# New places for activations and weights, and another order in the output projection, in a decoder layer that works with split float32

## The chip, the cores and the metric

The kernel runs on one core of one Trainium2 chip. The metric is the device time of one execution in microseconds: the median of three runs before the change is 1117.33 us (1116.82 to 1117.43). One more execution was profiled; all rows below are of that one.

## What is computed

One layer of a decoder, 256 tokens by 2048 channels, all float32. Cut to what matters here:

```python
h = rms_norm(x, ln_mix_pre[l])
proj = h @ w_in[l]                          # 2048 x 5648
q, k, v, z, xbc, dt_raw = jnp.split(proj, splits, axis=-1)
attn = moba_attention(...)                  # 8 heads of 128, one block of 256 tokens
ssm = mamba2_mixer(z, xbc, dt_raw, ...)     # 16 heads of 64, chunks of 128
mixed = jnp.concatenate([attn, ssm], axis=-1) @ w_out[l]    # 2048 x 2048
x = x + rms_norm(mixed, ln_mix_post[l])
h = rms_norm(x, ln_ffn_pre[l])
u = causal_depthwise_conv(h @ w_ffn_up[l], ...)             # 2048 x 11264
gate, up = jnp.split(u, [FFN_HIDDEN], axis=-1)
f = (jax.nn.gelu(gate, approximate=True) * up) @ w_ffn_down[l]   # 5632 x 2048
x = x + rms_norm(f, ln_ffn_post[l])
```

## The kernel before

**Split numbers.** Every large product is made of three: each weight and each activation is split into a part rounded to float32r ("hi") and the float32r rest ("lo"), and hi x hi, hi x lo and lo x hi are summed in PSUM. ACT rounds a weight (`whi`, L75), DVE subtracts (`wlo`, L76).

**Weights.** They come as 384 units of 128 x 1024 float32 (512 KB) in the order of use. `Weights.fetch` loads one (SP's queue, four `raw` buffers), rounds it and takes the rest. There are four buffers each for `whi` and `wlo`, and three more of each from the output projection on (`deepen`). Every unit used calls `tick`, which fetches the next unit and runs what `defer` has put off by a number of units.

**Two kinds of stages.** In a *column tile* (`cols_part`, L221 and L222; input projections of attention and part of the state-space model, and the FFN's up projection) a 128 x 128 block of the weight is loaded into the array and the activation streams: hi and lo together, 2 x 256 columns, against `whi`, then hi alone against `wlo`. Sixteen such pairs, two units, make one tile of 128 output channels. `cols_tok` (L229, L232) does the same for 128 tokens at a time, for the three tiles that begin while the second half of the tokens is not ready yet. In a *row stage* (`rows_part`, L284 to L286; v and z, the output projection, the FFN's down projection) a block of the activation is loaded and 512 columns of the weight stream; one unit gives 12 matmuls (two blocks of channels, two halves of the tokens, three products).

**Places.** The normalized activations `hT` and, for the FFN, `h2` are one tile of 128 x 16 x 2 x 256: for each block of channels, hi and then lo. The mixer's output `mT` and the gated FFN activation `gT` are two tiles each (`halves`), the lo one 32 float32 (`SHIFT`) further within 256 bytes. `Weights.place` puts the same shift ahead of the `wlo` buffers of each pool:

```python
        if n == "wlo" and pool not in self.shifted:
            self.shifted.append(pool)
            pool.tile([P, SHIFT], F32, name="gap")
```

**Order.** A scheduler orders ACT's and DVE's work by the order in which the code records it, except in the tail of the output projection, which is written by hand. The output projection has four chunks of 512 output channels. When a chunk's sums are complete, `post` squares them on ACT (for the norm), multiplies them by the norm weights on DVE (L768, L760) and makes one product of x with the next norm's weights (`x_weighted`, L763) for the second half of the tokens. Four more such products are deferred by 2 to 5 units. `rows_chunk` calls `done=post(c)` behind the last `tick` of the chunk, so behind the next unit's cast.

Of the kernel before, what the change touches and what calls it, by code (L numbers as in the profile page):

```python
# [19 lines left out]
P = 128  # L20
D = 2048
S = 256
# [33 lines left out]
class Weights:  # L56


    def __init__(self, nc, pool, units):
        self.nc, self.pool, self.units = nc, pool, units  # L60
        self.fetched, self.ready, self.more, self.base, self.behind = 0, [], None, 0, 0
        self.shifted = []

# [15 lines left out]
    def place(self, i, n, bufs, dtype):  # L79
        pool = self.pool  # L80
        if self.more and (i - self.base) % (bufs + MORE[n]) < MORE[n]:
            pool, bufs = self.more, MORE[n]
        if n == "wlo" and pool not in self.shifted:
            self.shifted.append(pool)
            pool.tile([P, SHIFT], F32, name="gap")
        return pool.tile([P, UE], dtype, name=n, tag=n, bufs=bufs)
# [35 lines left out]
def decoder_layer(ctx, tc, x, xT, win, wdt, wout, wup, wdown, relb, vec, cols, mconv, fconv,  # L122
# [11 lines left out]
    def pad(pool, name, n):  # L134
        pool.tile([P, n], F32, name=name)

    def halves(pool, name, n):

        lo = pool.tile([P, n, S], F32R, name=name + "l")
        pad(pool, name + "p", SHIFT)  # L140
        return [pool.tile([P, n, S], F32R, name=name + "h"), lo]

    def views(pair):

        return [pair[:, :, c, :] for c in range(2)]

# [6 lines left out]
    def tok(t):  # L153
        return slice(t * P, (t + 1) * P)
# [51 lines left out]
    def split_evac(dst, k, ts, ps):  # L206

        hi, lo = (d[:, k, ts] for d in dst)
        nc.scalar.copy(hi, ps)
        nc.vector.tensor_tensor(lo, ps, f32(hi), op=ALU.subtract)  # L210

    def split_scaled(dst, k, ts, src, w):

        hi, lo = (d[:, k, ts] for d in dst)
        nc.scalar.activation(hi, src, AF.Copy, scale=w)
        nc.vector.scalar_tensor_tensor(lo, src, w, f32(hi), op0=ALU.mult, op1=ALU.subtract)

    def cols_part(ps, w, aT, k, j):

        s = tok(j)  # L220
        nc.tensor.matmul(ps, w[0][:, s], aT[:, k, :, :], start=(k == 0), stop=False)  # L221
        end[0] = nc.tensor.matmul(ps[:, :S], w[1][:, s], aT[:, k, 0, :], start=False,  # L222
                                  stop=(k == KT - 1)).ins

    def cols_tok(ps, w, aT, k, j, t):

        s = tok(j)
        both = ps.rearrange("p (b c) -> p b c", b=2)[:, :, tok(t)]
        nc.tensor.matmul(both, w[0][:, s], aT[:, k, :, tok(t)], start=(t == 0 and k == 0),  # L229
                         stop=False)  # L230
        if t == NT - 1:
            nc.tensor.matmul(ps[:, :S], w[1][:, s], aT[:, k, 0, :], start=False,  # L232
                             stop=(k == KT - 1))
# [8 lines left out]
    def defer(units, fn, *args):  # L242

        pending.append([units, fn, args])
# [31 lines left out]
    def chunk_psums():  # L276
        return [acc.tile([P, 512], F32, name="pa", tag="a") for _ in range(NT)]

    def rows_part(ps, w, aT, k0, t, first, last):

        for j in range(2):
            s = chunk(j)
            a, b = (d[:, k0 + j, tok(t)] for d in aT)
            nc.tensor.matmul(ps, a, w[0][:, s], start=(first and j == 0), stop=False)  # L284
            nc.tensor.matmul(ps, a, w[1][:, s], start=False, stop=False)  # L285
            end[0] = nc.tensor.matmul(ps, b, w[0][:, s], start=False,  # L286
                                      stop=(last and j == 1)).ins

    def rows_chunk(pss, aT, kts, first=True, last=True, done=None):

        n = len(kts)
        for i in range(n):
            w = ws.take()
            for t in range(NT):
                rows_part(pss[t], w, aT, kts[i], t, first and i == 0, last and i == n - 1)
            tick()
        if done:
            for t in range(NT):
                done(t, pss[t])
# [37 lines left out]

    pad(pers, "pad0", 32)
    hT = pers.tile([P, KT, 2, S], F32R, name="hT", tag="h", bufs=1)
    pad(pers, "pad1", 32)  # L340

    with ExitStack() as mctx:
        mx = mctx.enter_context(tc.tile_pool(name="mx", bufs=1))
        mT = halves(mx, "mT", KT)

        with ExitStack() as actx:
# [7 lines left out]
            def load_x(g, n):  # L354
                nc.sync.dma_start(out=xr[:, g:g + n, :], in_=xT[:, g:g + n, :])
                for k in range(g, g + n):
                    split_scaled(views(hT), k, slice(0, S), xr[:, k, :], lnm[:, k:k + 1])

# [269 lines left out]
            for c in range(2):  # L628
                rows_chunk(chunk_psums(), views(hT), range(0, KT, 2), done=v_out(c))

# [93 lines left out]
            for c in range(2):  # L724
                rows_chunk(chunk_psums(), views(hT), range(0, KT, 2), done=gate(c))
            for h in range(2, H):
# [11 lines left out]
        for t in range(NT):  # L738
            aux(out=xt[:, t, :], in_=x[0, tok(t), :])
        pad(ctx.enter_context(tc.tile_pool(name="end", bufs=1, side="right")), "pad2", 16)  # L740
        ws.deepen(ctx.enter_context(tc.tile_pool(name="wq", bufs=1, side="right")))
# [13 lines left out]
        ss1 = pers.tile([P, NT, 4], F32, name="ss1")  # L755
        h2 = pers.tile([P, KT, 2, S], F32R, name="h2", tag="h", bufs=1)

# [7 lines left out]
        def post(c):  # L765
            def fn(t, ps):
                square_sum(ss[0][t][:, c:c + 1], ps)
                nc.vector.tensor_tensor(mm[:, t, chunk(c)], ps, wpost[:, chunk(c)], op=ALU.mult)  # L768
                weighted(t, c)
                if t == NT - 1:  # L770
                    x_weighted(t, c)
            return fn
# [22 lines left out]
        def turned(t, q):  # L795

            pt = psum("pxt").rearrange("p (j c) -> p j c", c=P)
            for j in range(4):
                nc.tensor.transpose(pt[:, j, :], ml[t][q][:, tok(j)], ident)
            dst = [h2[:, q * 4:q * 4 + 4, c, tok(t)] for c in range(2)]  # L800
            last = [nc.scalar.copy(dst[0], pt).ins]

            def rest():
                last.append(nc.vector.tensor_tensor(dst[1], pt, f32(dst[0]), op=ALU.subtract).ins)
            return rest, last
# [8 lines left out]

        for c in range(3):
            defer(2 + c, x_weighted, 0, c)
        defer(5, x_weighted, 1, 3)
        for c in range(2):
            rows_chunk(first[c], mT, hi, first=False, done=post(c))
        both = list(lo) + list(hi)  # L820
        rows_chunk(chunk_psums(), mT, both, done=post(2))
        early = [early_sum(ss[0][t][:, :3]) for t in range(NT)]
# [102 lines left out]
    fp = ctx.enter_context(tc.tile_pool(name="fp", bufs=1))  # L925
    gT = halves(fp, "gT", HALF)
    fcv = fp.tile([P, 2 * NF, 4], F32, name="fcv")
# [199 lines left out]
```

## Time and profile before

| | before |
|---|---|
| median of three runs | 1117.33 us |
| the profiled execution's own time | 1117.19 us |
| its span, first to last instruction | 1115.4 us |
| PE busy | 1108.2 us (99%) |
| DVE, ACT busy | 784.1 us (70%), 592.2 us (53%) |
| granted PE clock, mean | 0.999 |
| read from HBM | 214.44 MB |

PE's matmuls are pipelined: each is on record for longer than the distance to the next one's start. The rate is read from starts in the timeline, not from durations. "idle before" in a row is time in which the engine did nothing, and the name behind the arrow is what ended it.

### The profile page before, as it was taken

The page shows a single profiled execution, that of the slowest core. Times are in us where ns is not written, and L with a number is a line of the kernel's source. Part 1 is how long each engine was busy: PE and PEld are TensorE (multiplying, and loading weights), DVE is VectorE, ACT ScalarE, POOL GpSimd, SP SyncE. Part 2 cuts the span into 40 slices and gives each one's busy share as a digit, 9 for nine tenths or more (in the row PEclk, how much of TensorE's full clock was granted, in tenths as well). Part 3 has the DMA queues.
Part 4 walks back from the last instruction along what each step waited for, and adds up shares of the span by engine and source line. Part 5 has one row for each costly group of instructions (what it writes and reads, how often), then busy time and mean ns, then how long its engine had stood idle before and what let it go on. Part 6 is the DMA issues. An engine that isn't in the chain of part 4 may idle for free.

```text
span 1115.4 us, 15788 instructions
## 1 busy us (share of the span) xinstructions
PE 1108.2 (99%) x5888; PEld 946.6 (85%) x5888; DVE 784.1 (70%) x1270; ACT 592.2 (53%) x914; POOL 15.5 (1%) x26
## 2 busy tenths in 40 slices
PE   9999999999999999999999999999999999999997
PEld 7888888888888988888888888888888888888886
DVE  6699976776576799878777644448787878765553
ACT  6666545545454486555555444335555555554441
POOL 0010000000000000000000000000000000000000
PEclk9999999999999999999999999999999999999999
DMA  8758554555687267666556665666655656566542
GB/s 299 291 183 272 176 152 165 175 172 167 217 301 236 87 223 238 192 191 191 189 189 189 189 189 189 190 189 190 190 190 191 191 190 192 188 223 196 191 151 76
DMA packets 61356, 217.58 MB, mean 195 GB/s; under 512 B 7200, under 2 KB 8624, under 8 KB 60384
## 3 DMA queue, kind: packets, MB, share of 16 engines
q1 hardware_dynamic: 59328, 207.64, 57.6%
q0 software_dynamic: 1664, 8.59, 2.2%
q8 instruction: 46, 0.75, 0.3%
q10 hardware_dynamic: 288, 0.35, 0.1%
q14 instruction: 30, 0.25, 0.1%
HBM read 214.44 MB, written 2.11 MB: 194 GB/s over the span
## 4 chain that ended last, share of the span: by engine, by line
PE 98%; DMA 0%; SPq 0%; ACT 0%; DVE 0%; issue 0%; POOLq 0%; ACTq 0%
PE pa L221 36%; PE pa L222 18%; PE pa L285 9%; PE pa L284 9%; PE pa L286 9%; PE ph L285 4%; PE ph L284 4%; PE ph L286 4%; PE pab L221 1%; PE pa L229 1%; PE pab L222 1%; PE py L585 1%; DMA raw<-in_win_dram 0%; PE pq L229 0%; PE pa L232 0%; PE lg L675 0%
## 5 line engine op out<-in xcount | busy, mean ns | idle before, releaser
L76 DVE TENSOR_TENSOR wlo<-raw,whi 128x1024 fp32r<-128x1024 f32 (+2 forms) x389 | 469.5, 1210 | 256.9 <-ACT whi L75 249.0
L75 ACT CAST whi<-raw 128x1024 fp32r<-128x1024 f32 (+2 forms) x389 | 403.5, 1039 | 428.8 <-PE pa L221 198.2
L221 PE MATMUL pa<-h,whi 128*128 128x512 f32 x1360 | 471.7, 392 | 0.0
L222 PE MATMUL pa<-h,wlo 128*128 128x256 f32 x1360 | 382.2, 281 | 0.0
L221 PEld LDWEIGHTS pa<-h,whi 128*128 128x128 f32 x1360 | 255.3, 188 | 55.9
L222 PEld LDWEIGHTS pa<-h,wlo 128*128 128x128 f32 x1360 | 255.7, 188 | 0.0
L221 PE MATMUL pa<-hT,whi 128*128 128x512 f32 x384 | 136.7, 398 | 0.0
L222 PE MATMUL pa<-hT,wlo 128*128 128x256 f32 x384 | 107.0, 281 | 0.2 <-DVE wlo L76 0.2
L221 PEld LDWEIGHTS pa<-hT,whi 128*128 128x128 f32 x384 | 72.1, 188 | 15.7 <-issue 0.2
L943 DVE SCALAR_TENSOR_TENSOR cfc<-cfu,fcv,cfc 128x254 f32<-128x254 f32 (+1 forms) x176 | 83.2, 478 | 1.4
L222 PEld LDWEIGHTS pa<-hT,wlo 128*128 128x128 f32 x384 | 72.0, 188 | 1.2 <-DVE wlo L76 0.7
L285 PE MATMUL pa<-wlo,gTh 128*128 128x512 f32 x176 | 69.6, 396 | 0.0
L285 PE MATMUL ph<-wlo,gTh 128*128 128x512 f32 x176 | 69.6, 396 | 0.0
L284 PE MATMUL pa<-whi,gTh 128*128 128x512 f32 x176 | 69.0, 392 | 0.0
L284 PE MATMUL ph<-whi,gTh 128*128 128x512 f32 x176 | 69.0, 392 | 0.0
L286 PE MATMUL pa<-whi,gTl 128*128 128x512 f32 x176 | 68.9, 392 | 0.0
L286 PE MATMUL ph<-whi,gTl 128*128 128x512 f32 x176 | 68.9, 392 | 0.0
L941 ACT ACTIVATE cfc<-cfu,fcv 128x256 f32<-128x256 f32 x88 | 52.3, 599 | 0.2 <-DVE cfu L940 0.2
L284 PE MATMUL pa<-whi,hT 128*128 128x512 f32 x128 | 51.7, 404 | 0.0
L284 PE MATMUL pa<-whi,mTh 128*128 128x512 f32 x128 | 50.7, 396 | 0.0
L285 PE MATMUL pa<-wlo,mTh 128*128 128x512 f32 x128 | 50.6, 395 | 0.0
L286 PE MATMUL pa<-whi,hT 128*128 128x512 f32 x128 | 50.5, 394 | 0.0
(230 smaller groups left out, 1131.4 us busy)
## 6 DMA issues: line engine op xcount, KB each, us to landing
raw<-in_wup_dram SPq DMA_DIRECT2D x176, 512.0 KB, 3.5
raw<-in_wdown_dram SPq DMA_DIRECT2D x88, 512.0 KB, 3.5
raw<-in_win_dram SPq DMA_DIRECT2D x85, 512.0 KB, 3.7
raw<-in_wout_dram SPq DMA_DIRECT2D x32, 512.0 KB, 4.0
xsq<-in_x_dram SPq DMA_DIRECT2D x2, 1024.0 KB, 9.3
rows<-acd POOLq DMA_DIRECT2D x4, 512.0 KB, 8.0
xt<-in_x_dram POOLq DMA_DIRECT2D x2, 1024.0 KB, 6.8
xr<-in_xT_dram SPq DMA_DIRECT2D x6, 256.0 KB, 6.3
```

The source lines that it names most:

```text
L75: nc.scalar.copy(hi[:, s], raw[:, s])
L76: return lambda: nc.vector.tensor_tensor(lo[:, s], raw[:, s], f32(hi[:, s]), op=ALU.subtract)
L221: nc.tensor.matmul(ps, w[0][:, s], aT[:, k, :, :], start=(k == 0), stop=False)
L222: end[0] = nc.tensor.matmul(ps[:, :S], w[1][:, s], aT[:, k, 0, :], start=False, stop=(k == KT - 1)).ins
L229: nc.tensor.matmul(both, w[0][:, s], aT[:, k, :, tok(t)], start=(t == 0 and k == 0), stop=False)
L284: nc.tensor.matmul(ps, a, w[0][:, s], start=(first and j == 0), stop=False)
L285: nc.tensor.matmul(ps, a, w[1][:, s], start=False, stop=False)
L286: end[0] = nc.tensor.matmul(ps, b, w[0][:, s], start=False, stop=(last and j == 1)).ins
L585: nc.tensor.matmul(py[:, i * 64:(i + 1) * 64], rows[:, t, g, i, :], xcs[t, g][:, i * 64:(i + 1) * 64], start=True, stop=True)
L941: nc.scalar.activation(c, u, AF.Identity, scale=wv[:, 2:3], bias=wv[:, 3:4])
L943: nc.vector.scalar_tensor_tensor(c[:, sh:], u[:, :S - sh], wv[:, 2 - sh:3 - sh], c[:, sh:], op0=ALU.mult, op1=ALU.add)
```

## The change

`hT` and `h2` become two planes of 16 x 256 columns, each followed by 32 float32 of room, with the lo plane first; the first pad grows by 32 float32, so that plane 0 (lo) starts 160 bytes and plane 1 (hi) 32 bytes past a multiple of 256. The shift ahead of `wlo` is gone. `mT` and `gT` become one tile each, hi and lo side by side for each block of channels. In `cols_part` the lo summand streams first, then hi, and the matmul with `wlo` adds into the second half of the PSUM row. In the output projection, `post` is called ahead of the last `tick` of a chunk (`soon`), and the products of x are deferred by 9 to 14 units instead of 2 to 5.

```diff
@@ Weights
-        if n == "wlo" and pool not in self.shifted:
-            self.shifted.append(pool)
-            pool.tile([P, SHIFT], F32, name="gap")
...
-    def halves(pool, name, n):
-        lo = pool.tile([P, n, S], F32R, name=name + "l")
-        pad(pool, name + "p", SHIFT)
-        return [pool.tile([P, n, S], F32R, name=name + "h"), lo]
...
@@ cols_part
         s = tok(j)
-        nc.tensor.matmul(ps, w[0][:, s], aT[:, k, :, :], start=(k == 0), stop=False)
-        end[0] = nc.tensor.matmul(ps[:, :S], w[1][:, s], aT[:, k, 0, :], start=False,
+        c = slice(k * S, (k + 1) * S)
+        nc.tensor.matmul(ps, w[0][:, s], aT[:, :, c], start=(k == 0), stop=False)
+        end[0] = nc.tensor.matmul(ps[:, S:], w[1][:, s], aT[:, 1, c], start=False,
                                   stop=(k == KT - 1)).ins
@@ cols_tok
-        nc.tensor.matmul(both, w[0][:, s], aT[:, k, :, tok(t)], start=(t == 0 and k == 0),
-                         stop=False)
+        c = k * S
+        nc.tensor.matmul(both, w[0][:, s], aT[:, :, c:c + S][:, :, tok(t)],
+                         start=(t == 0 and k == 0), stop=False)
...
@@ rows_chunk
-    def rows_chunk(pss, aT, kts, first=True, last=True, done=None):
+    def rows_chunk(pss, aT, kts, first=True, last=True, done=None, soon=None):
...
+            if soon and i == n - 1:
+                for t in range(NT):
+                    soon(t, pss[t])
             tick()
...
-    pad(pers, "pad0", 32)
-    hT = pers.tile([P, KT, 2, S], F32R, name="hT", tag="h", bufs=1)
-    pad(pers, "pad1", 32)
+    pad(pers, "pad0", 64)
+    def normed(name):
+        return pers.tile([P, 2, KT * S + SHIFT], F32R, name=name, tag="h", bufs=1)
+    def summands(aT):
+        if len(aT.shape) == 4:
+            return [aT[:, :, c, :] for c in range(2)]
+        return [aT[:, c, :KT * S].rearrange("p (k s) -> p k s", s=S) for c in (1, 0)]
+    hT = normed("hT")
...
-        mT = halves(mx, "mT", KT)
+        mT = mx.tile([P, KT, 2, S], F32R, name="mT")
...
-        pad(ctx.enter_context(tc.tile_pool(name="end", bufs=1, side="right")), "pad2", 16)
+        pad(ctx.enter_context(tc.tile_pool(name="end", bufs=1, side="right")), "pad2", 48)
...
-        h2 = pers.tile([P, KT, 2, S], F32R, name="h2", tag="h", bufs=1)
+        h2 = normed("h2")
...
-                if t == NT - 1:
+                if (t, c) == (1, 2):
                     x_weighted(t, c)
...
-            dst = [h2[:, q * 4:q * 4 + 4, c, tok(t)] for c in range(2)]
+            dst = [d[:, q * 4:q * 4 + 4, tok(t)] for d in summands(h2)]
...
-        for c in range(3):
-            defer(2 + c, x_weighted, 0, c)
-        defer(5, x_weighted, 1, 3)
+        for i, (t, c) in enumerate(((0, 0), (1, 0), (0, 1), (1, 1), (0, 2), (1, 3))):
+            defer(9 + i, x_weighted, t, c)
         for c in range(2):
-            rows_chunk(first[c], mT, hi, first=False, done=post(c))
+            rows_chunk(first[c], mT, hi, first=False, soon=post(c))
         both = list(lo) + list(hi)
-        rows_chunk(chunk_psums(), mT, both, done=post(2))
+        rows_chunk(chunk_psums(), mT, both, soon=post(2))
...
-    gT = halves(fp, "gT", HALF)
+    gT = fp.tile([P, HALF, 2, S], F32R, name="gT")
```

PE's order is the same row for row but for names. On DVE and ACT instructions move in the output projection alone. DVE before, from the last split of the attention's output to the second chunk's sums (`xl` and `lnrow` on the left are products of x, `mm`, `ml` and `wpost` those of the sums):

```order
L76 TENSOR_TENSOR wlo<-raw,whi 128x1024 x7
L763 TENSOR_TENSOR xl_3046<-xt,lnrow 128x512
L76 TENSOR_TENSOR wlo<-raw,whi 128x1024
L763 TENSOR_TENSOR xl_3046<-xt,lnrow 128x512 x2
L76 TENSOR_TENSOR wlo<-raw,whi 128x1024
L768 TENSOR_TENSOR mm<-pa,wpost 128x512 x2
L760 TENSOR_TENSOR ml_3045<-mm,lnrow 128x512
L760 TENSOR_TENSOR wpost<-mm,lnrow 128x512
L76 TENSOR_TENSOR wlo<-raw,whi 128x1024
L763 TENSOR_TENSOR lnrow<-xt,lnrow 128x512
L763 TENSOR_TENSOR xl_3048<-xt,lnrow 128x512
L76 TENSOR_TENSOR wlo<-raw,whi 128x1024 x2
```

The same place now:

```order
L75 TENSOR_TENSOR wlo<-raw,whi 128x1024 x7
L765 TENSOR_TENSOR xl_3042<-xt,lnrow 128x512
L75 TENSOR_TENSOR wlo<-raw,whi 128x1024
L770 TENSOR_TENSOR mm<-pa,wpost 128x512 x2
L762 TENSOR_TENSOR ml_3041<-mm,lnrow 128x512
L762 TENSOR_TENSOR wpost<-mm,lnrow 128x512
L75 TENSOR_TENSOR wlo<-raw,whi 128x1024
L765 TENSOR_TENSOR lnrow<-xt,lnrow 128x512
L75 TENSOR_TENSOR wlo<-raw,whi 128x1024
L765 TENSOR_TENSOR xl_3042<-xt,lnrow 128x512 x2
L75 TENSOR_TENSOR wlo<-raw,whi 128x1024
L765 TENSOR_TENSOR xl_3044<-xt,lnrow 128x512
```

Two products of x and one weight rest moved from ahead of the first chunk's sums (`mm`) to behind them. ACT before, from the negated norm weights (`wpost`) through the first three chunks (`junk` is the square of the sums):

```order
L745 ACTIVATE wpost<-wpost 128x2048
L75 CAST whi<-raw 128x1024
L204 ACTIVATE junk,ss_3049<-pa 128x512
L75 CAST whi<-raw 128x1024
L204 ACTIVATE junk,ss_3050<-pa 128x512
L75 CAST whi<-raw 128x1024 x3
L204 ACTIVATE junk,ss_3049<-pa 128x512
L75 CAST whi<-raw 128x1024
L204 ACTIVATE junk,ss_3050<-pa 128x512
L75 CAST whi<-raw 128x1024 x7
```

And now:

```order
L747 ACTIVATE wpost<-wpost 128x2048
L74 CAST whi<-raw 128x1024
L190 ACTIVATE junk,ss_3045<-pa 128x512
L190 ACTIVATE junk,ss_3046<-pa 128x512
L74 CAST whi<-raw 128x1024 x4
L190 ACTIVATE junk,ss_3045<-pa 128x512
L190 ACTIVATE junk,ss_3046<-pa 128x512
L74 CAST whi<-raw 128x1024 x8
```

The cast that stood between the two squares of a chunk now stands behind both.

## Rows read from the trace of the kernel before

**Rows 1.** The page, busy time of the engines, and the chain that ended last.
```profile
PE 1108.2 (99%) x5888; PEld 946.6 (85%) x5888; DVE 784.1 (70%) x1270; ACT 592.2 (53%) x914; POOL 15.5 (1%) x26
PE 98%; DMA 0%; SPq 0%; ACT 0%; DVE 0%; issue 0%; POOLq 0%; ACTq 0%
```

**Rows 2.** Waits of PE, whole span: us in total, times, longest.
```profile
PE pa L977 <- ACT diag L975: 1.6, 1, 1.6
PE idle L335 <- DVE zero L332: 1.1, 1, 1.1
PE pa L222 <- DVE wlo L76: 0.2, 1, 0.2
```

**Rows 3.** Timeline of PE, column tiles: start us, duration us, engine, line, operation.
```profile
499.87 0.39 PE L221 MATMUL pa<-h,whi 128*128 128x512 f32 x1
500.10 0.28 PE L222 MATMUL pa<-h,wlo 128*128 128x256 f32 x1
500.21 0.39 PE L221 MATMUL pa<-h,whi 128*128 128x512 f32 x1
...
599.01 0.39 PE L221 MATMUL pa<-h,whi 128*128 128x512 f32 x1
```

**Rows 4.** Windows: stretch, us, busy PE, PEld, DVE, ACT, POOL, PEclk, DMA share, GB/s.
```profile
500.00:600.00 100.00, 100.00 (x579) 88.13 (x578) 78.92 (x128) 57.99 (x91) 0.00 (x0) 1.00 0.61 190
107.00:118.00 11.00, 11.00 (x65) 9.62 (x64) 11.00 (x22) 6.27 (x10) 0.00 (x0) 1.00 0.63 191
300.00:320.00 20.00, 20.00 (x88) 16.27 (x87) 8.80 (x9) 8.34 (x8) 1.28 (x3) 1.00 0.92 371
```

**Rows 5.** Timeline of PE, the FFN's down projection (row stage).
```profile
640.26 0.40 PE L284 MATMUL pa<-whi,gTh 128*128 128x512 f32 x1
...
733.88 0.39 PE L284 MATMUL ph<-whi,gTh 128*128 128x512 f32 x1
734.10 0.39 PE L285 MATMUL ph<-wlo,gTh 128*128 128x512 f32 x1
...
734.56 0.40 PE L284 MATMUL ph<-whi,gTh 128*128 128x512 f32 x1
...
735.26 0.39 PE L284 MATMUL ph<-whi,gTh 128*128 128x512 f32 x1
```

**Rows 6.** Groups by line: count, busy us, mean ns; the third from L221 alone.
```profile
L221 PE MATMUL pa<-h,whi 128*128 128x512 f32 x1360 | 471.7, 392 | 0.0
L221 PE MATMUL pa<-hT,whi 128*128 128x512 f32 x384 | 136.7, 398 | 0.0
L221 PE MATMUL pab<-hT,whi x64: 390/393/587, 4.5 to 50.4; 128*128 128x512 f32 x64
L284 PE MATMUL pa<-whi,gTh 128*128 128x512 f32 x176 | 69.0, 392 | 0.0
L284 PE MATMUL pa<-whi,hT 128*128 128x512 f32 x128 | 51.7, 404 | 0.0
```

**Rows 7.** Timeline of the weight loads (PEld), beside the matmuls of rows 3.
```profile
500.10 0.19 PEld L221 LDWEIGHTS pa<-h,whi 128*128 128x128 f32 x1
500.22 0.19 PEld L222 LDWEIGHTS pa<-h,wlo 128*128 128x128 f32 x1
```

**Rows 8.** Timeline of PE, column tiles of the first half.
```profile
106.98 0.39 PE L221 MATMUL pa<-hT,whi 128*128 128x512 f32 x1
...
117.83 0.40 PE L221 MATMUL pa<-hT,whi 128*128 128x512 f32 x1
```

**Rows 9.** Timeline of PE, second tokens of the first three FFN tiles.
```profile
379.01 0.28 PE L232 MATMUL pa<-h,wlo 128*128 128x256 f32 x1
379.12 0.28 PE L229 MATMUL pa<-h,whi 128*128 128x256 f32 x1
```

**Rows 10.** Groups on DVE, 321 to 337 us: count, busy us, mean ns.
```profile
L763 DVE TENSOR_TENSOR lnrow<-xt,lnrow 128x512 f32<-128x512 f32 x2 | 1.4, 688 | 0.0
```

**Rows 11.** Waits, 280 to 400 us: us in total, times, longest.
```profile
ACT whi L75 <- DMA raw<-in_wout_dram: 19.6, 10, 5.1
ACT whi L75 <- PE pa L286: 8.7, 8, 1.7
```

More of the change, by code (lines that the diff above doesn't have):

```diff
@@ L61, in __init__ @@
         self.fetched, self.ready, self.more, self.base, self.behind = 0, [], None, 0, 0
-        self.shifted = []
     def deepen(self, pool):
@@ L135, in pad @@
         pool.tile([P, n], F32, name=name)
-    def halves(pool, name, n):
-        lo = pool.tile([P, n, S], F32R, name=name + "l")
-        pad(pool, name + "p", SHIFT)
-        return [pool.tile([P, n, S], F32R, name=name + "h"), lo]
-    def views(pair):
-        return [pair[:, :, c, :] for c in range(2)]
     def row_bcast(off, n):
@@ L206, in split_evac @@
     def split_evac(dst, k, ts, ps):
-        hi, lo = (d[:, k, ts] for d in dst)
+        hi, lo = (d[:, k, ts] for d in summands(dst))
         nc.scalar.copy(hi, ps)
@@ L212, in split_scaled @@
     def split_scaled(dst, k, ts, src, w):
-        hi, lo = (d[:, k, ts] for d in dst)
+        hi, lo = (d[:, k, ts] for d in summands(dst))
         nc.scalar.activation(hi, src, AF.Copy, scale=w)
@@ L228, in cols_tok @@
         both = ps.rearrange("p (b c) -> p b c", b=2)[:, :, tok(t)]
-        nc.tensor.matmul(both, w[0][:, s], aT[:, k, :, tok(t)], start=(t == 0 and k == 0),
-                         stop=False)
+        c = k * S
+        nc.tensor.matmul(both, w[0][:, s], aT[:, :, c:c + S][:, :, tok(t)],
+                         start=(t == 0 and k == 0), stop=False)
         if t == NT - 1:
-            nc.tensor.matmul(ps[:, :S], w[1][:, s], aT[:, k, 0, :], start=False,
+            nc.tensor.matmul(ps[:, S:], w[1][:, s], aT[:, 1, c:c + S], start=False,
                              stop=(k == KT - 1))
@@ L282, in rows_part @@
             s = chunk(j)
-            a, b = (d[:, k0 + j, tok(t)] for d in aT)
+            a, b = (d[:, k0 + j, tok(t)] for d in summands(aT))
             nc.tensor.matmul(ps, a, w[0][:, s], start=(first and j == 0), stop=False)
@@ L356, in load_x @@
                 for k in range(g, g + n):
-                    split_scaled(views(hT), k, slice(0, S), xr[:, k, :], lnm[:, k:k + 1])
+                    split_scaled(hT, k, slice(0, S), xr[:, k, :], lnm[:, k:k + 1])
             wdr = ax.tile([P, KT, SH], F32, name="wdr")
@@ L628, in decoder_layer @@
             for c in range(2):
-                rows_chunk(chunk_psums(), views(hT), range(0, KT, 2), done=v_out(c))
+                rows_chunk(chunk_psums(), hT, range(0, KT, 2), done=v_out(c))
             for f in range(4, 8):
@@ L724, in decoder_layer @@
             for c in range(2):
-                rows_chunk(chunk_psums(), views(hT), range(0, KT, 2), done=gate(c))
+                rows_chunk(chunk_psums(), hT, range(0, KT, 2), done=gate(c))
             for h in range(2, H):
```

## The prediction

> **What bounds the kernel now.** I read the page's busy times first. TensorE (PE) is busy for 1108.2 us of the 1115.4 us span, and 98% of the chain that ended last is PE work [rows 1]. The list of who waited for whom says it more sharply: in the whole execution PE waited 1.6 us near the end, 1.1 us at the start and 0.2 us for a weight rest [rows 2]. So DVE (70% busy), ACT (53%) and the transfers cost nothing where they stand; the time is the number of matmuls times the distance from one start to the next.
>
> That distance I took from the timeline, because a matmul's own duration overlaps the next one. In the first projection of the second half (column tiles), the L221 matmul (512 columns: both summands of the activation) and L222 (256 columns: the rounded part alone) alternate. From the L221 that starts at 499.87 to the one at 599.01 there are 286 pairs in 99.14 us: 0.3466 us a pair, about 0.23 for the 512 columns and 0.117 for the 256 [rows 3]. The granted clock there is 1.00, the 2.4 GHz level [rows 4], at which 768 columns, one a cycle, take 0.3200 us. So 0.0266 us of each pair, 8%, is not streaming. In the row stages (weights stream, activations are the loaded operand) the L284 at 640.26 and the one at 733.88 are 405 matmuls of 512 columns apart: 93.62 us, 0.2312 each, against 0.2133 at that clock [rows 5], again 8% more.
>
> The kernel has 1360 + 384 + 64 = 1808 column pairs, 626.7 us at 0.3466, and 1824 row matmuls (each of L284, L285 and L286 twice 176 times with gT and 128 times each with mT and hT), 421.7 us at 0.2312 [rows 6]. The excess over streaming is 1808 x 0.0266 = 48.1 us and 1824 x 0.0179 = 32.6 us. Only this excess can move, for the change alters no column count.
>
> **The change, part by part.** *1. Layout of the column activations, all weights at one offset.* Row for row PE does the same matmuls in the same order; what differs is the address at which each operand starts. In the built programs (bytes, modulo 256) the activations and rounded weights start at 32 before, the weight rests at 160. After, rounded activations and all weights start at 32, the activation rests at 160. What can make an address cost time is a second reader. The weight load of the next matmul starts with the current one (loads at 500.10 and 500.22, matmuls at 500.10 and 500.21) and is on record for 0.19 us [rows 3, 7]. So I compared, for each kind of matmul, the start of the stream with the start of the load beside it:
> - L221: before 32 against 160, 128 apart; after, the stream begins with the rests: 160 against 32, 128 apart again.
> - L222: 32 against 32 both times.
> - Rows with gT and mT: equal offsets in all three matmuls, before (32/32, 160/160, 32/32) and after (32/32 three times).
> - Rows with hT: equal, 128 apart, equal, both times.
>
> So at the start of every load nothing changes. One thing does: a load lasts 0.19 us and 256 columns about 0.117, so the load of L221 runs some 0.07 us into the second plane, where the distance was 128 before and is 0 after. Bounds for the pair: from below the streaming time, 0.3200 [clock in rows 4]; from above the slowest steady pair on record, at 106.98 to 117.83: 31 pairs in 10.85 us, 0.3500 [rows 8]. I take 0.3466, unchanged, as the nearest row: the stages whose streams and loads are 128 apart in one matmul (columns) and in none (rows with gT) lie at the same 8% [rows 3, 5], so 128 bytes have no price of their own that I can see. Term: 0; ends -48.1 us (all 1808 pairs at 0.3200) and, for the 1744 pairs of the h and hT tiles, 1744 x 0.0034 = +5.9 us.
>
> The row stages get no new relation: 0. Their threes (L284 to the next L284) take turns there at 0.68 us, from 733.88 to 734.56, and 0.70, from 734.56 to 735.26 [rows 5]; the end below is all threes at the first (608 x -0.013 = -8 us), above all at the second (608 x 0.007 = +4 us), 0.693 being the mean.
>
> *2. The 144 matmuls of first and second tokens* (L229, L232) stream 2 x 128 columns from two planes instead of from one block: 0.12 us each before, as long as L222 [rows 9]. Term 0; a hundredth of a microsecond each way on each would be 1.4 us, and is my bound.
>
> *3. Splits into the new places.* ACT and DVE write the same shapes, and for h2 four pieces of 128 with half the step. Off PE's path, cover: DVE is 79% busy in the column stages, ACT 58% [rows 4]. Term 0. Without the cover (107 to 118 us, where DVE is busy for 11.00 of 11.00 us [rows 4]) PE still does not wait [rows 2].
>
> *4. The output projection's order.* Per chunk, ACT's two squares of the sums come before the next cast instead of around it, and of DVE's seven products of x with the norm weights two move from ahead of the first chunk's sums to behind them. No instruction is added or removed: 7 x 0.69 us of products on DVE [rows 10]. What is queued behind: an ACT square waits for the chunk's last matmul, and a cast that stood ahead of it now stands behind, at worst one unit (12 matmuls x 0.2312 = 2.8 us) later. Who waits: that cast's unit, some units later on PE. Cover: between 280 and 400 us eight casts wait for PE to give a buffer back [rows 11]; all seven weight buffers are full then, and the next use is several units of 2.8 us away. Where casts wait for the transfer of weights instead (19.6 us in ten waits [rows 11]), the cover is thinner, yet PE waited for none. Early release of the accumulators gains nothing, as PE waits for none of them [rows 2]. Term 0; ends 0 and +3 us (a cast one unit late with no cover).
>
> Sum: 1117.19 us, the profiled execution's own time (span 1115.4 and 1.8 around it), plus 0. It stands 0.1 under the median of the runs, 1117.33; I forecast 1117.3.
>
> **A rule against the trace.** The rows give 0.3466 us a pair, that is 0.027 beyond streaming, with a load beside every matmul [rows 3, 7]. The Trainium skill, TensorE: Matmul & The Clock Gate, Part 2 (What happens when you issue a matmul), step 1, says that PE has two independent SBUF read ports and that loading the next weights takes nothing from the running matmul; by that rule no offset matters and the change is worth 0. The same page, Part 1 (Wait, 56ns, not 53.3ns?), puts warm back-to-back starts at N / 2.4 + 2.5 ns; by that a pair would take 325 ns, which this trace does not reach anywhere. So the rows show an excess that the page does not explain.
>
> **The rivals.**
> - *Faster, in part (0.27).* The excess is the two readers meeting, and which plane streams while the load runs decides it. For: the excess has no other visible cause, and its size is not fixed by the columns alone (0.3466 and 0.3500 with the same layout [rows 3, 8]). Against: the same distance of 128 stands at the load's start before and after. If L221 loses half of its own excess (0.3466 - 0.117 - 0.2133 = 0.016), it is 1808 x 0.008 = 15 us: 1102; the closest starts of 512-column matmuls, 0.22 [rows 5], give the same size. A third of it gives 1107.
> - *Faster, by half of all excess or more (0.14).* The loads hide wholly, or almost: 24 to 48 of the 48.1 us, 1069 to 1093. Against: no stretch of this trace comes near it, and L222 looks bound by its load (after a 256-column matmul the next starts 0.11 or 0.12 us later in the column tiles and in the second tokens alike [rows 3, 9]). The formula of TensorE: Matmul & The Clock Gate in the Trainium skill, quoted above, lies in this case: 1808 x 0.0216 = 39 us, 1078, by an estimate from the page.
> - *Slower (0.16): columns fall into the slower rhythm.* With the old layout the pairs already run in two steady rhythms, 0.3466 and 0.3500; the slower one held for two tiles [rows 8]. The new stream jumps by a plane in the middle and meets equal offsets behind the jump. If the columns settle there: 1744 x 0.0034 = +5.9, 1123. It decides from 0.0012 us a pair on, since 1808 x 0.0012 is 2.2 us.
> - *Slower (0.06): the projection stalls.* A cast behind the moved squares comes late while the transfers are slow (DMA share 0.92 from 300 to 320 us [rows 4]); 3 us: 1120.
>
> **How the numbers follow.** Unchanged rhythm has 0.37, the largest single case, since every relation at a load's start is kept; its own range is 1115.5 to 1119. About 0.2%, 2.2 us, is what a measurement can tell from no change. Faster is 0.27 + 0.14 = 0.41, slower 0.16 + 0.06 = 0.22, same 0.37. The range goes from 1098 (half of L221's excess and a little of L222's) to 1124 (the slower rhythm); it leaves out the full gain and slower rhythms than any on record, less than 2 in 10.
>
> **What would show it.** Right: L221 starts still pair at 0.346 to 0.348 us around 500 us, row matmuls stay at 0.231, PE waits under 4 us in all, and the first second-half tile starts within 1 us of 391. Wrong in the first step: another pair distance between 400 and 610 us, the same in every tile. Wrong in the fourth: a PE wait for whi or wlo between 300 and 390 us.

## The result and the profile after

| | before | after |
|---|---|---|
| median (6 runs each, side by side) | 1117.38 us | 1110.91 us |
| lowest to highest | 1116.82 to 1118.02 | 1110.68 to 1113.07 |
| the profiled execution's own time | 1117.19 us | 1110.68 us |
| its span | 1115.4 us | 1108.6 us |

The change makes the kernel faster: after over before is 0.9947 (95% interval 0.9937 to 0.9958), 6.5 us. That is inside the predicted range (1098 to 1124), 6.4 us under the forecast of 1117.3, and on the side that I had given 0.41; the forecast itself was no change.

On the page of the kernel after, busy times first and the costliest groups behind them (line, engine, operation, names, count | busy us, mean ns | idle before), PE is busy for 99% of the span as in [rows 1], and the matmul counts of [rows 6] are the same:

```profile
PE 1101.4 (99%) x5888; PEld 945.5 (85%) x5888; DVE 784.2 (71%) x1270; ACT 593.1 (53%) x914; POOL 15.5 (1%) x26
...
L208 PE MATMUL pa<-h,whi 128*128 128x512 f32 x1360 | 471.7, 394 | 0.0
...
L272 PE MATMUL pa<-whi,gT 128*128 128x512 f32 x176 | 68.5, 389 | 0.0
```

PE's waits (us in total, times, longest) are those of [rows 2]:

```profile
PE pa L979 <- ACT diag L977: 1.6, 1, 1.6
PE idle L327 <- DVE zero L324: 1.1, 1, 1.1
PE pab L209 <- DVE wlo L75: 0.2, 1, 0.2
```

So no wait went and none came; what changed is how close the matmuls follow each other. PE's timeline after (start us, duration us) shows a column tile (L208 and L209, the old L221 and L222) and the down projection (L272 to L274, the old L284 to L286):

```profile
499.03 0.40 PE L208 MATMUL pa<-h,whi 128*128 128x512 f32 x1
499.26 0.28 PE L209 MATMUL pa<-h,wlo 128*128 128x256 f32 x1
...
598.18 0.40 PE L208 MATMUL pa<-h,whi 128*128 128x512 f32 x1
...
623.38 0.39 PE L272 MATMUL pa<-whi,gT 128*128 128x512 f32 x1
623.61 0.39 PE L273 MATMUL pa<-wlo,gT 128*128 128x512 f32 x1
...
691.38 0.39 PE L272 MATMUL ph<-whi,gT 128*128 128x512 f32 x1
```

The columns did not move: 286 pairs lie between 499.03 and 598.18, 0.3467 us each, as in [rows 3]. The row stage did: 300 matmuls between 623.38 and 691.38, 0.2267 us each, against 0.2312 in [rows 5]; a three (the matmuls of L272, L273 and L274, up to the next L272) takes 0.680 us, where before it took 0.693. The windows view (stretch, us, busy time and count of PE, PEld, DVE, ACT and POOL, then granted clock, DMA share, GB/s) shows the same clock for both kernels, the 2.4 GHz level as in [rows 4]. Two windows of the kernel before, then two of the kernel after:

```profile
775.47:879.47 104.00, 104.00 (x602) 91.67 (x601) 82.83 (x133) 60.22 (x95) 0.00 (x0) 1.00 0.61 192
625.72:695.05 69.33, 69.33 (x301) 56.30 (x300) 30.96 (x27) 28.53 (x30) 0.00 (x0) 1.00 0.60 189
```

```profile
770.94:874.94 104.00, 104.00 (x602) 91.32 (x601) 82.88 (x133) 60.23 (x95) 0.00 (x0) 1.00 0.60 191
623.38:691.38 68.00, 68.00 (x301) 56.31 (x300) 30.97 (x27) 28.76 (x30) 0.00 (x0) 1.00 0.61 193
```

A window here starts with the first matmul of a pair or three and ends where that of the 300th pair, or the 100th three, further on starts; its count takes in a matmul or two that overlap its edges. Unless said otherwise, windows come in such pairs, the first in the up projection, the second in the down projection: one divides the length of the first by 300 and that of the second by 100.

Summed from start to start over whole stages, the rows with gT went from 244.07 to 239.42 us, those with mT from 89.19 to 87.64, the FFN's columns from 489.2 to 489.1, the first half's columns from 159.5 to 159.0, and the rows with hT from 90.5 to 90.3. The two stages whose activations were two separate tiles give 6.2 of the 6.8 us by which the two spans differ. They have 352 + 128 = 480 threes, and 480 x 0.0133 us is 6.4: nearly the whole gain is one step of 0.0133 us, 32 cycles at this clock, in a three.

### The profile page after: what moved, and what is told of

It reads as the page before. It is cut to its first block, busy times and chain, and to the rows that moved or that the text cites. A ratio compares the mean times of both kernels' runs of the same rounds, so it can differ in the third digit from the quotient of the medians.

```text
span 1108.6 us, 15791 instructions
## 1 busy us (share of the span) xinstructions
PE 1101.4 (99%) x5888; PEld 945.5 (85%) x5888; DVE 784.2 (71%) x1270; ACT 593.1 (53%) x914; POOL 15.5 (1%) x26
## 4 chain that ended last, share of the span: by engine, by line
PE 98%; DMA 0%; SPq 0%; ACT 0%; DVE 0%; issue 0%; POOLq 0%; ACTq 0%
PE pa L208 36%; PE pa L209 18%; PE pa L274 9%; PE pa L273 9%; PE pa L272 9%; PE ph L272 4%; PE ph L273 4%; PE ph L274 4%; PE pab L208 1%; PE pa L217 1%; PE py L587 1%; PE pab L209 1%; DMA raw<-in_win_dram 0%; PE pa L220 0%; PE pq L217 0%; PE lg L677 0%
## 5 line engine op out<-in xcount | busy, mean ns | idle before, releaser
L208 PE MATMUL pa<-h,whi 128*128 128x512 f32 x1360 | 471.7, 394 | 0.0
L209 PE MATMUL pa<-h,wlo 128*128 128x256 f32 x1360 | 379.1, 279 | 0.0
L208 PEld LDWEIGHTS pa<-h,whi 128*128 128x128 f32 x1360 | 255.5, 188 | 57.4
L209 PEld LDWEIGHTS pa<-h,wlo 128*128 128x128 f32 x1360 | 255.3, 188 | 0.0
L208 PE MATMUL pa<-hT,whi 128*128 128x512 f32 x384 | 136.5, 399 | 0.0
L209 PE MATMUL pa<-hT,wlo 128*128 128x256 f32 x384 | 106.5, 279 | 0.0
L208 PEld LDWEIGHTS pa<-hT,whi 128*128 128x128 f32 x384 | 72.5, 189 | 15.6 <-issue 0.2
L209 PEld LDWEIGHTS pa<-hT,wlo 128*128 128x128 f32 x384 | 72.1, 189 | 0.5 <-issue 0.2
L272 PE MATMUL pa<-whi,gT 128*128 128x512 f32 x176 | 68.5, 389 | 0.0
L274 PE MATMUL pa<-whi,gT 128*128 128x512 f32 x176 | 68.5, 389 | 0.0
L274 PE MATMUL ph<-whi,gT 128*128 128x512 f32 x176 | 68.5, 389 | 0.0
L272 PE MATMUL ph<-whi,gT 128*128 128x512 f32 x176 | 68.5, 389 | 0.0
L273 PE MATMUL ph<-wlo,gT 128*128 128x512 f32 x176 | 68.5, 389 | 0.0
L273 PE MATMUL pa<-wlo,gT 128*128 128x512 f32 x176 | 68.5, 389 | 0.0
L272 PE MATMUL pa<-whi,hT 128*128 128x512 f32 x128 | 51.1, 399 | 0.0
L274 PE MATMUL pa<-whi,hT 128*128 128x512 f32 x128 | 50.8, 397 | 0.0
L273 PE MATMUL pa<-wlo,hT 128*128 128x512 f32 x128 | 50.7, 396 | 0.0
L272 PE MATMUL pa<-whi,mT 128*128 128x512 f32 x128 | 50.3, 393 | 0.0
```

What stands on the lines that cost most here:

```text
L208: nc.tensor.matmul(ps, w[0][:, s], aT[:, :, c], start=(k == 0), stop=False)
L209: end[0] = nc.tensor.matmul(ps[:, S:], w[1][:, s], aT[:, 1, c], start=False, stop=(k == KT - 1)).ins
L274: end[0] = nc.tensor.matmul(ps, b, w[0][:, s], start=False, stop=(last and j == 1)).ins
```

## The experiments

Offsets are bytes past a multiple of 256, of the first element that a matmul streams or loads. In a row stage the weights stream and the activations are loaded; in a column tile it is the other way round. The profiled execution of each run gives the threes (gT) and the pairs (FFN columns); the medians are over all its runs. Where two values stand, one part of the stage ran at the one and the rest at the other. A ratio is to the runs of the kernel before made beside it (medians 1117.04 for a1 to a4, 1117.59 for c1 to c4, 1117.39 for e1 and e2).

| run | whi, wlo | rows gT: hi, lo | columns: how they stream | three | pair | median | ratio to before |
|---|---|---|---|---|---|---|---|
| before | 32, 160 | 32, 160 | one block from 32 | 0.6933 | 0.3467 | 1117.38 | 1 |
| after | 32, 32 | 32, 32 | lo at 160, hi at 32 | 0.6800 | 0.3467 | 1110.91 | 0.9947 |
| a1 | 32, 160 | 32, 32 | as after | 0.6934 | 0.3533 and 0.3467 | 1123.78 | 1.0068 |
| a2 | 32, 32 | 32, 160 | as after | 0.6933 | 0.3467 | 1117.14 | 1.0003 |
| a3 | 32, 32 | 32, 32 | one block from 32 | 0.6800 | 0.3533 | 1121.62 | 1.0039 |
| a4 | 32, 32 | 32, 32 | as after | 0.6800 | 0.3467 | 1111.33 | 0.9957 |
| c1 | 160, 160 | 32, 32 | one block from 32 | 0.6971 | 0.3511 | 1126.13 | 1.0079 |
| c2 | 96, 96 | 32, 32 | one block from 32 | 0.6866 | 0.3533 | 1123.67 | 1.0057 |
| c3 | 32, 160 | 32, 32 | as after | 0.690 and 0.693 | 0.3533 and 0.3467 | 1123.09 | 1.0050 |
| c4 | 32, 32 | 32, 32 | hi at 160, lo at 32 | 0.6800 | 0.3533 | 1120.79 | 1.0029 |
| e1 | 32, 32 | 192, 192 | lo at 96, hi at 32 | 0.7000 | 0.3505 | 1127.16 | 1.0086 |
| e2 | 32, 32 | 0, 0 | hi at 32, lo at 160 | 0.7000 | 0.3500 | 1126.25 | 1.0086 |

**The change taken apart (a1 to a4).** The theory after the result: a row stage is fast only where all its streams and all its loads start at one offset. The rivals: the place of the weights alone does it, or that of the activations alone; and, for the columns, that planes are needed only because equal offsets of weights would harm them.

*a1: the weights' rests 128 bytes off again.* The kernel after with the old gap, and with pads (not shown) that leave the activations where they were:

```diff
+        if n == "wlo" and pool not in self.shifted:
+            self.shifted.append(pool)
+            pool.tile([P, SHIFT], F32, name="gap")
```

> The changed kernel, with the weight rests alone moved 128 bytes away again (activations as in the change). Theory one (a row stage is fast only where all three streams and all three loads of a three start at one offset modulo 256): the threes of the down projection go back from 0.680 to 0.693 us, 480 threes x 0.0133 = 6.4 us, time about 1117; columns unchanged at 0.3467 a pair. Rival two (only where the loaded activations lie matters): threes stay at 0.680, time 1111.

The time went to 1123.78 us, past the kernel before and past both expectations. Windows of a1, the third in the first half of the up projection (300 pairs):

```profile
777.18:883.18 106.00, 106.00 (x602) 90.92 (x601) 82.83 (x133) 59.69 (x94) 0.00 (x0) 1.00 0.58 188
626.76:696.10 69.34, 69.34 (x302) 56.35 (x300) 30.96 (x27) 28.56 (x30) 0.00 (x0) 1.00 0.59 191
427.09:531.09 104.00, 104.00 (x603) 91.29 (x601) 85.25 (x138) 61.44 (x97) 0.00 (x0) 1.00 0.62 201
```

The threes are back at 0.693 although activations and rounded weights all start together: one odd stream in three is enough, as theory one said. The columns, which it left unchanged, moved too: the first product's stream and the wlo load beside it now both start at 160, and in the second half of the up projection the pairs are at 0.3533. In its first half, with the same offsets, they stayed at 0.3467, so the offsets alone do not fix the time of a pair. From start to start the FFN's columns lose 4.9 us against after, the first half's 1.6, and the rows with mT and gT 6.3: 12.8, measured 12.9.

*a2: the activations' rests 128 bytes off, in tiles of their own, as before the change.*

```diff
-        mT = mx.tile([P, KT, 2, S], F32R, name="mT")
+        mT = halves(mx, "mT", KT)
...
-    gT = fp.tile([P, HALF, 2, S], F32R, name="gT")
+    gT = halves(fp, "gT", HALF)
```

> The changed kernel, with the rests of mT and gT alone 128 bytes away again, all weights at one offset. Theory one (uniform offsets): threes back to 0.693, time about 1117. Rival (only the streaming weights' offset matters): threes stay at 0.680, time 1111.

```profile
774.72:878.72 104.00, 104.00 (x603) 91.33 (x601) 82.84 (x133) 60.21 (x95) 0.00 (x0) 1.00 0.59 191
624.95:694.28 69.33, 69.33 (x302) 56.75 (x300) 30.95 (x27) 28.59 (x30) 0.00 (x0) 1.00 0.58 190
```

All of the gain is gone (1.0003, interval 0.9993 to 1.0012), as theory one said, and only the rows moved: one odd load in three costs the same 32 cycles as one odd stream (a1), and as both together (before). So neither part of the change gives the gain alone.

*a3: the kernel before with everything at 32, without planes* (the pad `pad2` follows).

```diff
-SHIFT = 32
+SHIFT = 64
```

> The kernel before with the shift of 256 bytes instead of 128, so that everything, hT and h2 too, starts at 32 modulo 256. Theory one with columns that don't care: rows at 0.680 in all stages, those with hT too, columns 0.3467 a pair: 1110.9 less 128 threes x 0.0133 = 1.7, about 1109. Rival three (the two planes 128 bytes apart are what keeps the columns at 0.3467): rows 0.680 but a column pair at 0.350 or more, 1808 x 0.0033 = 6 us or more on top, 1115 or above.

```profile
778.67:884.67 106.00, 106.00 (x602) 91.91 (x601) 82.85 (x133) 59.73 (x94) 0.00 (x0) 1.00 0.57 188
630.48:698.48 68.00, 68.00 (x302) 56.31 (x301) 30.95 (x27) 28.75 (x30) 0.00 (x0) 1.00 0.60 195
20.33:34.19 13.86, 13.86 (x82) 12.12 (x81) 9.04 (x15) 7.98 (x11) 0.00 (x0) 1.00 0.97 347
```

The rows have the gain, those with hT too (89.1 us against 90.5); mT and gT are still tiles of their own here, so it is the offset that counts and not the one tile. But the pairs went to 0.3533, and the FFN's columns to 498.3 us from 489.2: rival three. That is what the planes are good for: with all weights at one offset, the first product's stream no longer starts 128 bytes off its load, and the columns give back more than the rows gain. The planes put that distance back. Here too some tiles at the start ran at the old rhythm with the same offsets (third window, 40 pairs).

*a4: the kernel after with the old order in the output projection.*

```diff
-        for i, (t, c) in enumerate(((0, 0), (1, 0), (0, 1), (1, 1), (0, 2), (1, 3))):
-            defer(9 + i, x_weighted, t, c)
+        for c in range(3):
+            defer(2 + c, x_weighted, 0, c)
+        defer(5, x_weighted, 1, 3)
```

with `soon=` turned back into `done=` and the old condition in `post`.

> The changed kernel with the output projection's old order. Theory: the order is worth nothing, since PE waits for nothing there: 1111 within 1 us, PE waits as after. Rival: the faster rows need the new order, without it PE waits for weights or sums between 300 and 390 us: 1112 to 1115.

Its ratio of 0.9957 (0.9942 to 0.9971) can't be told from the kernel after's. PE's waits are as short in the new order and in the old; those of a4:

```profile
PE pa L980 <- ACT diag L978: 1.6, 1, 1.6
PE idle L327 <- DVE zero L324: 1.1, 1, 1.1
```

The new order is worth nothing that these runs can show.

**What the rule is, and whether it gives a better kernel (c1 to c4).** *c1 and c2* ask whether streams and loads must start at the same offset, or only each kind at one. They are the kernel before with one offset for all activations and another for all weights, 128 (c1) or 64 bytes (c2) further:

```diff
-        if n == "wlo" and pool not in self.shifted:
+        if n == "whi" and pool not in self.shifted:
             self.shifted.append(pool)
-            pool.tile([P, SHIFT], F32, name="gap")
+            pool.tile([P, 32], F32, name="gap")
...
+        pad(pool, name + "q", 32)
         lo = pool.tile([P, n, S], F32R, name=name + "l")
-        pad(pool, name + "p", SHIFT)
+        pad(pool, name + "p", 2 * SHIFT)
```

(In c2 the gap is 16, the pad `q` 48, and `pad2` follows.)

> The kernel before with every activation (columns' and rows', rounded and rest) at one offset of 256 bytes and both weight tiles 128 bytes off that. Theory A (a row stage pays 32 cycles more per three only where its streams differ among themselves or its loads differ among themselves; a column pair pays more only where the first product's stream and the load beside it start at one offset): 0.680 us a three in all three row stages, the attention's normed rows among them (610 threes by 0.0133 = 8.1 us), and 0.3467 us a column pair, so about 1109 us, ahead of the kernel after by 1.7. Theory B (what is needed in the rows is that stream and load start at the same offset): threes at 0.693, pairs at 0.3467, about 1117. Theory C (a distance of 128 bytes is no cure for columns by itself, the cure is that two streams alternate): pairs at 0.353, about 1116 to 1122.

> As the run with the weights 128 bytes off, with 64 bytes in place of 128. Theory A in its form 'any distance but none': as that run, rows 0.680, pairs 0.3467, about 1109 us. Form 'it has to be the other half of 256 bytes': pairs at 0.353 as with everything at one offset, about 1116 to 1122 us, rows as the run with 128 bytes shows.

Windows of c1, and then of c2:

```profile
781.81:887.14 105.33, 105.33 (x602) 92.31 (x601) 82.89 (x133) 59.83 (x94) 0.00 (x0) 1.00 0.57 189
630.98:700.69 69.71, 69.71 (x301) 56.52 (x300) 30.95 (x27) 28.51 (x30) 0.00 (x0) 1.00 0.58 189
```

```profile
778.98:884.98 106.00, 106.00 (x602) 92.06 (x601) 82.88 (x134) 59.77 (x94) 0.00 (x0) 1.00 0.58 187
629.67:698.33 68.66, 68.66 (x301) 56.34 (x300) 30.97 (x27) 28.55 (x30) 0.00 (x0) 1.00 0.60 191
```

Theory A fell: a uniform distance is no cure, and 1126.13 us (c1) is slower than any of the three theories gave. In the rows, 128 bytes cost more (0.697) than the mixture of before, and 64 bytes 0.687; B's condition, that stream and load start at the same offset, fits both runs (the kernel before shows that it is not enough by itself), but its figure of 0.693 was too low for c1. In the columns a distance for both products is bad too (0.351 and 0.353), where the kernels before and after have it for the first product alone.

*c3: a1 with the six products of a unit in an order with half as many changes of stream offset.*

```diff
+        six = [(a[0], 0, 0), (b[0], 0, 0), (a[0], 1, 0), (a[1], 1, 1), (a[1], 0, 1), (b[1], 0, 1)]
```

> The run a1 (rests of the weights 128 bytes off) with the six row products of a weight unit in the order rounded, rounded, rest | rest, rounded, rounded, so that the stream changes its offset twice per six in place of four times; the number of loads stays at six. If the added 32 cycles of a three hang on a change of offset from one stream to the next, six products take some 1.373 us in place of 1.387 (480 + 130 threes, half of 8.1 us: 4 us less than a1's 1123.8, about 1120). If they hang on the stream that stands at the odd offset, whatever went before: 1.387 as a1, about 1124. Columns as in a1, mixed 0.3467 and 0.3533, in both cases.

Windows of c3, both in the down projection (100 threes each), in its first and in its second half:

```profile
627.11:696.44 69.33, 69.33 (x301) 56.30 (x300) 30.98 (x27) 28.51 (x30) 0.00 (x0) 1.00 0.58 190
1000.16:1069.16 69.00, 69.00 (x302) 56.30 (x300) 36.92 (x35) 31.71 (x37) 0.00 (x0) 1.00 0.59 193
```

Six products took 1.380 us with mT, between the two expectations, and with gT 1.387 in the first half and 1.380 in the second; the time, 1123.09 us, is 0.7 us from a1's, less than either kernel's runs spread. The run does not settle whether the change of offset or the odd stream costs; a reading that fits mT here, c1's rows with mT (0.700) and a1 is 16 cycles for a stream 128 bytes off its load and 8 for each change of offset from one stream to the next. With the changes from one load to the next counted as well, at 8 too, it also gives the 0.693 of before and a2; it misses c1's rows with gT (0.697 in place of 0.700) and the first half of c3's. It was put together afterwards, and no run tests it.

*c4: the kernel after with hi and lo planes exchanged,* so that the second product of a pair streams 128 bytes off its load.

```diff
-        return [aT[:, c, :KT * S].rearrange("p (k s) -> p k s", s=S) for c in (1, 0)]
+        return [aT[:, c, :KT * S].rearrange("p (k s) -> p k s", s=S) for c in (0, 1)]
...
-        end[0] = nc.tensor.matmul(ps[:, S:], w[1][:, s], aT[:, 1, c], start=False,
+        end[0] = nc.tensor.matmul(ps[:, :S], w[1][:, s], aT[:, 0, c], start=False,
```

> The kernel after with the two planes of the normed tiles exchanged: rounded parts 128 bytes off the weights, rests at the weights' offset. The second product of a column pair then streams 128 bytes off the load beside it, where in the kernel after it streams at the load's offset. If only the first product's distance matters: pairs at 0.3467, 1111 us as the kernel after. If each product pays for a load at its own offset: less than 0.3467 a pair (up to 16 cycles, 0.0067 us, by 1411 + 459 pairs: 12 us, about 1099 us). If the odd stream is what costs: 0.353, about 1121 us. The normed rows (130 threes) stay at 0.693.

```profile
777.33:883.33 106.00, 106.00 (x602) 91.27 (x601) 82.90 (x133) 59.78 (x94) 0.00 (x0) 1.00 0.58 188
629.12:697.12 68.00, 68.00 (x301) 56.31 (x300) 30.96 (x27) 28.80 (x30) 0.00 (x0) 1.00 0.60 193
392.29:402.69 10.40, 10.40 (x62) 9.08 (x61) 9.78 (x19) 7.54 (x16) 0.72 (x1) 1.00 0.68 236
```

The first product is as in the kernel after, yet the pairs are at 0.3533, the figure of the third expectation: with these offsets the second product does worse 128 bytes off its load. Not in every tile, though: the third window, 30 pairs at the start of the second half of the layer, is at 0.3467 with the same offsets. The whole loss (9.9 us against after) is in the columns, but for about 1 us in rows.

**Other distances (e1, e2).** Both are the kernel after with mT and gT moved as a whole, and with another start of the first column product.

```diff
-    pad(pers, "pad0", 64)
+    pad(pers, "pad0", 48)
...
-        return pers.tile([P, 2, KT * S + SHIFT], F32R, name=name, tag="h", bufs=1)
+        return pers.tile([P, 2, KT * S + 48], F32R, name=name, tag="h", bufs=1)
...
+        pad(mx, "padm", 16)
...
+    pad(fp, "padg", 40)
```

That is e1; more pads (not shown) leave what lies behind in its place.

> The kernel after with other distances: the rests of the normed columns 64 bytes off their rounded plane in place of 128, the merged heads (mT) 64 bytes above the weights, the gated units (gT) 96 bytes below them. Theory D (a load costs the stream beside it 32 cycles where both start at one offset of 256 bytes and more at any distance, 48 at 128): threes on mT and gT between 0.683 and 0.70 us (480 threes by 0.003 to 0.02: 1.4 to 9.6 us more than the kernel after). Its rival (some distance other than 0 is better still): below 0.680 on one of the two. Columns: 0.3467 us a pair if any distance of the first product's stream from its load will do, up to 0.353 (12 us more) if it has to be half of 256 bytes. In all 1112 to 1133 us by theory D.

e2 exchanges the planes as c4 does and places them so that hi stays at 32, with mT at 64 and gT at 0.

> The kernel after with the rounded plane first in the first column product's stream (it starts at the weights' offset and goes over to the rests, 128 bytes off, after 256 columns; the second product streams the rounded plane as in the kernel after), mT 32 bytes above the weights and gT 32 bytes below. If the offset at the stream's start counts, as with the load that begins there: pairs at 0.353, 12 us more than the kernel after. If the half that streams later counts: 0.3467. Rows: threes between 0.681 and 0.69 by theory D (0.5 to 5 us more), below 0.680 by its rival. In all 1111 to 1128 us.

Windows of e1, and then of e2:

```profile
782.18:887.32 105.14, 105.14 (x602) 92.20 (x601) 82.91 (x133) 59.91 (x95) 0.00 (x0) 1.00 0.58 189
630.93:700.93 70.00, 70.00 (x302) 56.31 (x301) 30.94 (x27) 28.62 (x30) 0.00 (x0) 1.00 0.57 188
```

```profile
780.63:885.63 105.00, 105.00 (x603) 91.59 (x602) 82.87 (x133) 59.88 (x94) 0.00 (x0) 1.00 0.58 189
629.43:699.43 70.00, 70.00 (x302) 56.23 (x300) 30.99 (x27) 28.50 (x30) 0.00 (x0) 1.00 0.59 188
```

With mT and gT alike, four distances (64 bytes above the weights, 96 below, 32 above, 32 below) give 0.700 us a three, more than I had expected for the small ones: 48 cycles a matmul beyond its 512 columns, in place of 32. That fits theory D, which has a price for any distance, and its rival has nothing for it. But D names only distances, and the kernel before, with none, took 0.693. The pairs came out between, 0.3505 and 0.3500: in e2 the first product streams the same 512 columns as in the kernel after, only begun at the other plane, and the pairs are slower; in e1 it begins 64 bytes off its load, and they are slower too. Nothing tried beats the kernel after.

## Why the prediction was right or wrong

**The step that failed** is the sentence "The row stages get no new relation: 0". It measured 6.2 us (480 threes by some 0.013). I compared each stream only with the load beside it and found equal offsets before and after (32/32, 160/160, 32/32), so I expected nothing. The runs show that this comparison is not enough: a three in which stream and load move off together (before), the stream alone (a1) or the load alone (a2) costs 0.693 us each time, and 0.680 only where all start together (after, a3, c4). The end that I gave the term, -8 us, was 0.013 a three for 608 threes; 480 of them took that step. That the size fits is luck: I read it from the shorter of two threes that took turns, and had no reason why all should become as short. The 128 with hT did not, since the planes leave their rests at 160 (0.693 after); a3 shows that they would.

That 1110.9 lies in the range is luck too: the range came from gains and losses of the columns, which did not move, and was wide enough for a gain in a term that I had put at 0.

**"128 bytes have no price of their own that I can see"** was wrong. I read it from two kinds of stages that both lose 8%, but that likeness hid a difference: columns were already at the best found in any run, rows were not.

**Columns, 0:** right in size, 0.3467 both times. Its ground, that the distance at each load's start is kept, is borne out in part by a3 and c4, where it is not kept and a pair costs 0.0067 us more in most tiles; in some, as in half of a1's up projection, it costs nothing. The jump between planes, from which I had drawn both a gain and a loss, changed nothing. The slower rhythm of [rows 8] did not spread; the first half's columns, where it was, came out 0.5 us shorter.

**Projection order, 0, and splits, 0:** right (a4; PE's waits unchanged). **First and second tokens, 0:** right; their 144 matmuls take 17.6 us from start to start in both kernels.

**The rivals.** "Faster, in part" had the sign and the kind of cause (a stream and a load that meet), but put it into L221 and from its excess made 1102; the gain was in the rows and came to 1110.9. Of the signs to look for, the pair distance and the waits came out as for no change. The row matmuls did not stay at 0.231, and the first full tile of the second half started at 388.91 us, 2.1 before the 391 that I had named: that is the gain with mT (1.6) and some half a microsecond ahead of it.

**The rule weighed.** The Trainium skill, TensorE: Matmul & The Clock Gate, Part 2 (What happens when you issue a matmul), step 1, has loading the next weights take no SBUF read bandwidth from the running matmul. By that rule alone the places of loads and streams could not matter to each other. The runs disagree: with the same matmuls and loads, the places alone move the time from 1110.91 (after) to 1127.16 us (e1), and in a2 the loaded operands of the rows alone move and cost the whole gain.

## What to carry to other kernels

Where PE never waits and yet its starts are further apart than its columns, compare the offsets of all operands of a repeated group, not only of neighbours in time, and try one common offset for everything; a stage in which the load is the weight and one in which it is the activation may want different places. Change the places of one operand kind alone only with a measurement: half of this change gives nothing (a2) or costs 12.9 us against the whole (a1). A term that stands at 0 between two ends of one stage's own rhythm (0.68 and 0.70 here) deserves a chance of its own.

## What was not expected of the hardware

- Even at the best places found a 512-column row matmul takes 0.2267 us from start to start with a load beside it, 544 cycles for 512 columns; in 12 kernels no row stage went below that. With other places a three took 0.687 to 0.700 us, where this rate gives 0.680.
- It is not the distance between stream and load that counts alone: a three took 0.687 us with the weights 64 bytes above the activations (c2) and 0.700 with the activations 64 above (e1, mT).
- The 768 columns of a pair take 0.3467 us at best, when the 512-column stream starts 128 bytes off its load and the 256-column stream at its load's offset; the other places tried took 0.350 to 0.353 us in most tiles. But a1, a3 and c4 each ran some tiles at 0.3467 with the very offsets that gave 0.3533 in others, and c3's rows with gT had two rhythms too, so something besides the offsets takes part; what, and whether it is the same in every execution, stays open, as one execution of each kernel was profiled. How the cost of an odd stream divides between itself and the change (c3) is open as well.
